# A two-layer encoder whose mixer order comes from a recorded plan: other prices for switches and narrow products, two other hand-over times

## The chip, the cores and the metric

The program runs on one core of one Trainium2 chip. The time is the device time of one execution in microseconds; the median of the runs is compared. The engines are TensorE (PE, with its weight loads as PEld), VectorE (DVE), ScalarE (ACT), GpSimd (POOL) and SyncE (SP, which issues most of the loads).

## The reference

The kernel computes two layers on a sequence of 512 positions and 1024 channels in float32, then a last RMS norm. `x` below is the residual stream.

```python
for layer in range(2):
    xn = rms_norm(x, mix_norm[layer])
    x = x + (fox_diff_mixer(xn) if layer == 0 else mlstm_mixer(xn))
    x = x + memory_cross_attention(rms_norm(x, ...), rms_norm(mem, ...), wq, wkv, wo)
    x = x + conv_ffn(rms_norm(x, ...), w_up, conv_w, conv_b, w_down)
return rms_norm(x, final_norm)
```

The first mixer has four heads of differential attention (two score maps each, one subtracted from the other) and eight heads of attention with a decay that is cumulated along the sequence; their outputs are joined and go through one output projection. The second mixer is an mLSTM of four heads. `mem` has 256 positions.

## The kernel before

Activations lie transposed: channels on the 128 partitions, the 512 positions along the free dimension, in eight tiles. Each float32 matrix product of a projection is made of three products of a faster kind (`float32r`): both operands are split into a rounded part and a rest (`wh` and `wl`, `xh` and `xl`), ACT casts the rounded part and DVE subtracts it (L655 is the line of the recording wrapper, so that nearly every instruction carries it, and tiles tell them apart). Loads of weights (`raw`) are issued by SP, three buffers deep.

Products of the other kind, plain float32, are few: transposes by the identity (`w<-ident,x`), probabilities times values (`w<-pt,v`) and some sums over columns. The text calls these narrow and the `float32r` products wide, as the planner does. The differential heads' `w<-pt,v` fill all 128 columns; those of the decaying heads come in pairs, two 64-column halves of the array, each with a `tile_position`.

A head of the first mixer runs like this. Two projections give queries and keys; DVE scales them (`tmp`), ACT and DVE write the parts `qa`, `ka`, `kb` in halves of 64 partitions. For each of four blocks of queries PE makes the scores (`s<-ka,qa`, `s<-kb,qa`) in one of two banks `s`; a DVE instruction (`x<-s,dmask` or `x<-s,tb`, named ISA in lists of the order and CUSTOM_DVE_ANT_0 in the trace) adds the mask or the decay and takes the row minimum, which frees the bank; ACT takes the exponential with its sum; DVE normalizes (`x<-x,sm`); PE transposes; DVE or ACT copies the result to `pt`; PE multiplies by the values. For the decaying heads POOL makes the mask (`tb<-fb`, an affine select) from the cumulated decays, which come from a chain of eight-row DVE instructions and a scan (`tmp<-ones,mem`) and go through memory (`decays`, `fb`). Meanwhile the memory input is prepared (`sq`, `sqt`, `mem`) for the cross-attention, and products of its key projection (`acc<-mem,wh`, `acc<-mem,wl`), which depend on nothing in the mixer, are put between the heads' work as fill. The heads' work ends at about 199 us on PE; the output projection (`acc<-mh,wh` and so on) follows.

The order of all this within a mixer is not written by hand. `Plan` first lays out the large steps by priorities (`PROJ`, `SOFT`). A `Recorder` notes every instruction that the steps issue, gives each a duration (`cost`), and hands the list to `Sched`, a list scheduler with one clock for each engine: `run` picks, engine by engine, the instruction that can start first or nearly so, by due times (`dues`). PE's tasks are due when the recorder's own clock reaches them, less an amount in `EARLIES` for each head. `again` first runs the schedule once and then makes PE's start times the due times of a second run. The instructions are then issued in the order found, and each engine carries its own out in that order. Times of the plan are used for nothing else: where the plan's clock is wrong, the chip waits.

For the prices, `cost` gives a wide product `MM * n / 512` with `MM = 0.216` us and a least value, and a narrow one four times that; a factor stands for products with a `tile_position`. In `Sched.run`, `self.kind` tells that the product before was narrow, `t.kinds` the kind of a task's first and last product, and `SWITCH = 0.083` us is what a change of kind adds. `DECAY_AT` is the time in the plan before which the decays' chain is not begun. Both mixers use these prices (the second has its own `EARLIES1` and no decays of this form).

Of the kernel before, what the change touches and what calls it, by code (L numbers as in the profile page):

```python
# [29 lines left out]
X_AT, X_STEP = 2.6, 0.6  # L30
WARM = 10
ROW_DMA, SPREAD_DMA, LATE = 2.7, 6.0, 12.0
DECAY_AT = 70
MEM_AT, MEM_STEP = (100, 20), (4.0, 4.0)
FILLS, FILL_AT, FILL_PRIO = 2, (130.0, 100.0), 99
FILL_DUE, FILL_LAST = ((215.0, None), (None, None)), (2, 0)
# [143 lines left out]
MM = 0.216  # L180
# [5 lines left out]
SWITCH = 0.083  # L186
# [14 lines left out]
PROJ = [10, 55, 30, 57, 64, 73, 73, 73]  # L201
SOFT = [-29, 17.5, 40.5, 23.0, 30.5, -4.5, 41.0, 156.5]
FV = [55]
EARLIES = [177.0, 102.0, 114.0, 56, 54.0, 114.0, 152, 57.0]
PROJ1, SOFT1, NORM1 = [1, -30, 20, 33], [3, 19.5, 30.5, 90], [0, 66.5, 79.5, 8.0]
GATE1, V1 = [33, 34, -24, 51], [-42, 20]
EARLIES1 = [30.0, 96.0, 105.0, 87.0, 60.0, 129.0, 90.0, 111.0]
# [9 lines left out]
class Sched:  # L217
# [66 lines left out]
    def run(self):  # L284
        if self.wait or self.exact:
            self.dues()
        order = sorted(self.tasks, key=lambda t: (t.prio, t.n))
        todo = {}
        want = {r: [] for r in self.slots}
        for t in order:  # L290
            todo.setdefault(t.eng, []).append(t)
        for t in self.tasks:
            for r, _ in t.take if not t.loose else ():
                want[r].append(t)
        now = {e: -self.ahead.get(e, 0.0) for e in todo}
        inf = float("inf")
        idle = 0.0
        while any(todo.values()):
            best = None
            for e, ts in todo.items():  # L300
                able = []
                for t in ts if e == "-" else ts[:300]:
                    at = max(t.after, -99.0 if e == "-" else now[e])
                    ok = True
                    for d in t.deps:
                        if d.end is None:
                            ok = False
                            break
                        at = max(at, d.end + (d.same if d.eng == e else d.lat))
                    if not ok:  # L310
                        continue
                    for j, (r, _) in enumerate(t.take):
                        if not t.loose and want[r][0] is not t:
                            ok = False
                            break
                        at = max(at, self.slots[r][self.slot(r, sum(a == r for a, _ in t.take[:j]))])
                    if not ok or at == inf:
                        continue
                    able.append((at, t))
                if able:  # L320
                    near = min(at for at, _ in able) + self.wait.get(e, 0.0) + 1e-6
                    soon, pick = next((at, t) for at, t in able if at <= near)
                    if best is None or soon < best[0]:
                        best = (soon, e, pick)
            assert best is not None, [(e, t.n, t.prio, [d.n for d in t.deps if d.end is None], t.take) for e, ts in todo.items() for t in ts[:3]]
            at, e, t = best
            todo[e].remove(t)
            if e == "PE":
                idle += at - now[e]
            if t.table and t.table != self.table:  # L330
                self.table, t.dur = t.table, t.dur + TABLE
            if t.kinds:
                if self.kind and t.kinds[0]:
                    t.dur += SWITCH
                self.kind = not t.kinds[1]
            t.start, t.end = at, at + t.dur
            now[e] = t.end
            for r, st in t.take:
                if not t.loose:
                    want[r].pop(0)  # L340
                s = self.slot(r)
                self.turn[r] += 1
                self.slots[r][s] = inf
                st["_" + r] = s
            for r, st in t.free:
                self.slots[r][st["_" + r]] = t.end + 0.1
            if t.fn:
                t.fn()
        self.now, self.idle = now, idle
# [108 lines left out]
class Recorder:  # L458
# [35 lines left out]
    def item(self, t, it):  # L494
        prio = it.prio
        self.last, self.it, it.tasks = None, it, []
        self.early = EARLIES[SOFT.index(prio)] if prio in SOFT and not self.layer else EARLIES1[(SOFT1 + NORM1).index(prio)] if self.layer and prio in SOFT1 + NORM1 else 0.0
        if self.direct and t >= self.at:
# [11 lines left out]
    def cost(self, eng, name, out, a, k):  # L510
        n = int(np.prod(out.shape[1:])) if not isinstance(out, View) or out.idx is not None else 0
        if name == "dma_start":
            return (0.0017 * n, 3.3) if eng == "sync" else (0.57 if eng == "gpsimd" else 0.36, 2.8 if n < 512 or out.shape[0] < P else 4.0)
        if eng == "tensor":
            if name == "transpose":
                return 0.109, 0.2
            rhs = k.get("rhs", a[2] if len(a) > 2 else None)
            n = int(np.prod(rhs.shape[1:]))
            wide = (rhs.ref.dtype if isinstance(rhs, View) else rhs.dtype) == F32R
            return (max(0.11, MM * n / 512) if wide else max(0.22, 4 * MM * n / 512)) * (0.7 if "tile_position" in k else 1.0), 0.2  # L520
        if eng == "vector":
            two = 0.065 + 1.06e-3 * n
            if name == "tensor_tensor_reduce":
                return two, 0.25
            if name == "scalar_tensor_tensor":
                return two + (0.06 if isinstance(k["scalar"], View) or not isinstance(k["scalar"], (int, float)) else 0.0), 0.25
            if name == "tensor_tensor":
                return two + (0.02 if n == 512 else 0.0), 0.25
            if name == "tensor_tensor_scan":
                return 1.13, 0.25  # L530
            if name in ("tensor_copy", "reciprocal"):
                return 0.07 + 1.03e-3 * n, 0.25
            if name == "tensor_scalar":
                return (0.07 if isinstance(k["scalar1"], float) else 0.135) + 0.53e-3 * n, 0.25
            if name == "tensor_reduce":
                return 0.2, 0.25
            return 0.1 + 0.85e-3 * n, 0.25
        if eng == "scalar":
            d = 0.1 + 0.83e-3 * n + (0.07 if name == "copy" and n == 512 else 0.0)
            if any(k.get(w) is not None and not isinstance(k[w], float) for w in ("scale", "bias")):  # L540
                d += 0.09
            if isinstance(out, View) and out.idx is not None and len(out.shape) == 3 and out.shape[2] == 4:
                d += 0.42
            return d + (0.1 if "accum_out" in k else 0.0), 0.25
        return {"affine_select": 0.14 + 0.85e-3 * n, "tensor_tensor": 1.3, "memset": 0.1}.get(name, 0.1), 0.25
# [143 lines left out]
class Builder:  # L689
# [630 lines left out]
    def mix0(self):  # L1320
        nc, t, tc = self.nc, self.t, self.tc
        with tc.tile_pool(name="mix0", bufs=1, reuse_waits="tile") as mp:
# [94 lines left out]
            g = self.p_gate(pl, lambda: gw, 40, gates, xk, [norm], 1)  # L1417
            g = pl.add(decays, 0, [g], 1, take=("ta", "ta"), free=("ta", "ta"), chain=(("A", 1.0), ("D", 0.6), ("A", 0.5), ("D", 3.4), ("-", ROW_DMA)), after=DECAY_AT)

# [1579 lines left out]
```

## Time and profile before

| | |
|---|---|
| median of 3 runs | 1389.02 us (1388.33 to 1389.69) |
| the profiled execution | 1388.45 us, span of its core 1386.7 us |
| PE busy | 1376.9 us (99%) |
| DVE, ACT, POOL busy | 1196.1, 883.6 and 153.3 us |
| granted TensorE clock | 1.00 throughout |

The page and the views give times in us from the start of the span. Matmuls overlap: a row's second number is how long a product took from its start to its modelled end, 0.38 us for 512 columns, while the next one starts 0.216 us later. Waits of PE therefore show as a distance between the starts of two rows that is longer than usual, and only for the longest as idle time in brackets.

### The profile page before, as it was taken

Reading aid. Unit: us, or ns where it says so; the run is one execution under the profiler, and the core shown is the slowest. Engines: PE = TensorE matmul, PEld = TensorE weight load, DVE = VectorE, ACT = ScalarE, POOL = GpSimd, SP = SyncE. Lnnn points to the kernel's source line nnn. Section 1 sums busy time; section 2 is a strip of 40 time slices with the busy share of each in tenths; the row PEclk is TensorE's granted clock in tenths of the full one; section 3 lists DMA queues with packets and bytes.
Section 4 is the critical chain, followed back from the end, with each engine's and each line's share of the span. In section 5 each row is a group of like instructions: output and inputs, shape, how many; then the busy total and the mean of one; then the engine's idle time right before and its main releaser. Section 6 shows DMA issues by size and latency. Waiting matters only on the chain.

```text
span 1386.7 us, 23590 instructions
## 1 busy us (share of the span) xinstructions
PE 1376.9 (99%) x8846; PEld 1263.1 (91%) x8846; DVE 1196.1 (86%) x2061; ACT 883.6 (64%) x1517; POOL 153.3 (11%) x213
## 2 busy tenths in 40 slices
PE   9999999999999999999999999999999999999998
PEld 8888888899899999999888889889989999999997
DVE  7887886887899999999768889678879999999984
ACT  7887764766667665666447675466656765665555
POOL 0012310010011111010001221001001111010000
PEclk9999999999999999999999999999999999999999
DMA  6243343865468777683353243477464887766622
GB/s 209 76 138 92 115 135 101 266 175 168 140 171 204 194 195 184 157 200 101 104 175 111 92 132 115 145 205 224 145 171 135 197 210 196 181 174 172 153 75 77
DMA packets 85410, 215.29 MB, mean 155 GB/s; under 512 B 11072, under 2 KB 11584, under 8 KB 85296
## 3 DMA queue, kind: packets, MB, share of 16 engines
q1 hardware_dynamic: 67104, 169.09, 37.0%
q0 software_dynamic: 15904, 43.44, 17.8%
q8 instruction: 69, 1.13, 0.3%
q10 hardware_dynamic: 2288, 1.26, 0.3%
q14 instruction: 45, 0.37, 0.1%
HBM read 205.30 MB, written 8.44 MB: 154 GB/s over the span
## 4 chain that ended last, share of the span: by engine, by line
PE 92%; DVE 6%; ACT 1%; issue 1%; POOLq 0%; ACTq 0%; DVEq 0%
PE acc L655 62%; PE w L655 17%; PE s L655 12%; DVE wl L655 1%; DVE x L655 1%; DVE sm L655 1%; DVE qc L655 1%; DVE f L655 1%; DVE va L655 1%; ACT ka L655 0%; ACT x L655 0%; DVE k L655 0%; DVE xe L655 0%; ACT qc L655 0%; DVE sa L655 0%
## 5 line engine op out<-in xcount | busy, mean ns | idle before, releaser
L655 ACT CAST wh<-raw 128x1024 fp32r<-128x1024 f32 (+2 forms) x218 | 222.2, 1022 | 154.2 <-PE acc L655 102.5
L655 DVE TENSOR_TENSOR wl<-raw,wh 128x1024 fp32r<-128x1024 f32 (+2 forms) x218 | 259.2, 1191 | 30.3 <-ACT wh L655 29.6
L655 PE MATMUL acc<-xh,wh 128*128 128x256 f32 (+1 forms) x704 | 228.8, 325 | 0.2 <-DVE x L655 0.2
L655 PE MATMUL acc<-xh,wl 128*128 128x256 f32 (+1 forms) x704 | 227.1, 323 | 0.0
L655 PE MATMUL acc<-xl,wh 128*128 128x256 f32 (+1 forms) x704 | 226.9, 322 | 0.0
L655 PEld LDWEIGHTS acc<-xh,wl 128*128 128x128 f32 x704 | 134.3, 191 | 8.5
L655 PEld LDWEIGHTS acc<-xh,wh 128*128 128x128 f32 x704 | 134.3, 191 | 8.3 <-DVE x L655 0.6
L655 PEld LDWEIGHTS acc<-xl,wh 128*128 128x128 f32 x704 | 134.4, 191 | 7.6
L655 DVE SCALAR_TENSOR_TENSOR qc<-va,vec,qc 128x512 f32<-128x512 f32 x176 | 131.8, 749 | 6.2 <-ACT qc L655 3.5
L655 PE MATMUL acc<-f,k 128*128 128x256 f32 x1008 | 126.1, 275 | 0.0
L655 PE MATMUL w<-q,wh 128*128 128x512 f32 x416 | 123.9, 380 | 0.3 <-ACT qc L655 0.3
L655 PEld LDWEIGHTS acc<-f,k 128*128 128x128 f32 x1008 | 121.5, 192 | 1.7
L655 PE MATMUL acc<-mem,wh 128*128 128x256 f32 (+1 forms) x472 | 103.2, 313 | 0.0
L655 ACT ACTIVATE qc<-va,vec 128x512 f32<-128x512 f32 x88 | 71.4, 814 | 32.1 <-DVE va L655 19.8
L655 ACT ACTIVATE u<-acc 128x256 f32<-128x256 f32 x96 | 36.6, 382 | 76.8 <-PE acc L655 70.7
L655 PEld LDWEIGHTS w<-q,wh 128*128 128x128 f32 x416 | 75.4, 190 | 9.5 <-ACT qc L655 0.7
L655 PEld LDWEIGHTS acc<-mem,wh 128*128 128x128 f32 x472 | 78.4, 191 | 4.7
L655 PE MATMUL w<-q,wl 128*128 128x512 f32 x208 | 78.9, 379 | 0.0
L655 PE MATMUL acc<-mem,wl 128*128 128x256 f32 (+1 forms) x236 | 73.8, 313 | 0.0
L655 DVE TENSOR_TENSOR x<-acc,x 128x512 f32<-128x512 f32 (+1 forms) x43 | 28.0, 654 | 47.5 <-PE acc L655 47.5
L655 PE MATMUL acc<-f,wh 128*128 128x256 f32 x384 | 66.8, 275 | 0.0
L655 PE MATMUL s<-f,wh 128*128 128x256 f32 x384 | 66.8, 275 | 0.0
(382 smaller groups left out, 3501.7 us busy)
## 6 DMA issues: line engine op xcount, KB each, us to landing
raw<-in_up_dram SPq DMA_DIRECT2D x46, 512.0 KB, 4.1
raw<-in_down_dram SPq DMA_DIRECT2D x32, 512.0 KB, 4.1
sa<-in_up_dram SPq DMA_DIRECT2D x28, 512.0 KB, 4.7
sa<-in_up_dram POOLq DMA_DIRECT2D x28, 512.0 KB, 6.3
vb<-in_up_dram SPq DMA_DIRECT2D x42, 256.0 KB, 3.9
xe<-in_up_dram POOLq DMA_DIRECT2D x42, 256.0 KB, 4.7
raw<-in_xk_dram SPq DMA_DIRECT2D x16, 512.0 KB, 3.9
raw<-in_wo_dram SPq DMA_DIRECT2D x16, 512.0 KB, 3.4
```

Source lines behind the costliest of these rows:

```text
L655: i = issue(*map(real, a), **{w: real(v) for w, v in k.items()})
```

## The change

Four things are edited. A switch of product kind costs the planner 0.083 us when PE goes from narrow to wide, as before, and now gives back 0.083 us when it goes from wide to narrow. The least duration of a wide product becomes 0.1115 us, and the factor for products with a `tile_position` 0.55 where it was 0.7. The decays may begin at 40 us in the plan where they could at 70. The third differential head's amount in `EARLIES` becomes 117 where it was 114.

```diff
-DECAY_AT = 70
+DECAY_AT = 40
...
-EARLIES = [177.0, 102.0, 114.0, 56, 54.0, 114.0, 152, 57.0]
+EARLIES = [177.0, 102.0, 117.0, 56, 54.0, 114.0, 152, 57.0]
...
             if t.kinds:
-                if self.kind and t.kinds[0]:
-                    t.dur += SWITCH
+                t.dur += SWITCH * ((self.kind and t.kinds[0]) - (not self.kind and not t.kinds[0]))
                 self.kind = not t.kinds[1]
...
-            return (max(0.11, MM * n / 512) if wide else max(0.22, 4 * MM * n / 512)) * (0.7 if "tile_position" in k else 1.0), 0.2
+            return (max(0.1115, MM * n / 512) if wide else max(0.22, 4 * MM * n / 512)) * (0.55 if "tile_position" in k else 1.0), 0.2
```

No instruction is added or removed on any engine; PE has 8756 products in both programs. PE's order is the same up to about 53 us of the trace and from about 199 us on; in the second mixer PE's order stays, and a handful of instructions on DVE, ACT, POOL and SP change places with a neighbour.

ACT, second differential head, at 56 to 62 us of the trace of before. The `ka` are its keys, `pt` the probabilities of the first head on their way to PE, `wh` a weight's rounded part, `sq`, `sqt` and `mem` the memory's preparation. First as it stood:

```order
L655 CAST wh_667<-raw_502 128x1024
L655 ACTIVATE sq_685<-raw_542 128x256
L655 ACTIVATE x_142<-x_142,sm_641 128x512
L655 CAST ka_126_692<-tmp_670 64x512
L655 CAST ka_127_700<-tmp_670 64x512
L655 CAST ka_126_692<-tmp_670 64x512
L655 CAST ka_127_700<-tmp_670 64x512
L655 ACTIVATE sqt_717<-raw_542 128x256
L655 ACTIVATE mem_722<-raw_542,vec 128x256
L655 COPY pt_633<-w_712 128x3x128
```

And as it stands after the change:

```order
L654 CAST ka_126_680<-tmp_674 64x512
L654 CAST ka_128_692<-tmp_674 64x512
L654 ACTIVATE x_142<-x_142,sm_648 128x512
L654 CAST ka_126_680<-tmp_674 64x512
L654 CAST ka_128_692<-tmp_674 64x512
L654 CAST wh_711<-raw_502 128x1024
L654 COPY pt_635<-w_716 128x3x128
L654 ACTIVATE x_136,sm_721<-x_136,sm_721 128x128
L654 ACTIVATE x_135,sm_731<-x_135,sm_731 128x128
L654 ACTIVATE sq_745<-raw_546 128x256
L654 ACTIVATE sqt_747<-raw_546 128x256
L654 ACTIVATE mem_751<-raw_546,vec 128x256
```

The three instructions of the memory's preparation went behind the copy to `pt`; the weight's cast stays ahead of it.

DVE, decaying heads, at 164 to 168 us. The ISA rows evict scores of the banks `s`, the row of `sm` behind each is its second half; `wl` is a weight's rest, `tmp<-acc` a scaled projection. As it stood:

```order
L655 ISA x_137,sm_1933<-s_1895,tb_1919 128x256
L655 ISA sm_1933 128x1
L655 RECIPROCAL sm_1880<-sm_1880 128x1
L655 COPY pt_1625<-w_1914 128x128
L655 TENSOR_SCALAR x_142<-x_142,sm_1880 128x512
L655 TENSOR_TENSOR wl_1952<-raw_1661,wh_1912 128x1024
L655 ISA x_139,sm_1965<-s_1949,tb_1937 128x384
L655 ISA sm_1965 128x1
L655 ISA x_140,sm_1969<-s_1954,tb_1944 128x512
```

After the change:

```order
L654 ISA x_139,sm_1937<-s_1893,tb_1930 128x256
L654 ISA sm_1937 128x1
L654 SCALAR_TENSOR_TENSOR tmp_1945<-acc_387_1817,rb_377 128x512
L654 COPY pt_1787<-w_1939 128x128
L654 ISA x_137,sm_1964<-s_1951,tb_1947 128x384
L654 ISA sm_1964 128x1
L654 ISA x_140,sm_1974<-s_1955,tb_1958 128x512
```

Between the eviction of 256 columns and that of 384 the weight's subtraction and a scaling of 512 columns are gone (they stand earlier now), and a scaled projection stands there.

PE, last decaying heads, at 185 to 188 us: scores among the fill. As it stood:

```order
L655 MATMUL acc_480_2245<-mem_807,wh_2109 128x256 x2
L655 MATMUL acc_480_2245<-mem_807,wl_2154 128x256
L655 MATMUL w_2270<-ident,x_141 128x128
L655 MATMUL acc_480_2245<-mem_820,wh_2109 128x256 x2
L655 MATMUL s_2266<-ka_455_2118,qa_435_2017 128x256
L655 MATMUL s_2266<-kb_112,qa_435_2017 128x256
```

After the change, from the last score ahead of such a place on:

```order
L654 MATMUL s_2232<-kb_114,qa_435_2024 128x256
L654 MATMUL acc_458_2128<-mem_837,wh_1915 128x256 x2
L654 MATMUL acc_458_2128<-mem_837,wl_2148 128x256
L654 MATMUL acc_458_2128<-mem_844,wh_1915 128x256 x2
L654 MATMUL acc_458_2128<-mem_844,wl_2148 128x256
L654 MATMUL acc_458_2128<-mem_889,wh_1915 128x256 x2
L654 MATMUL acc_458_2128<-mem_889,wl_2148 128x256
L654 MATMUL acc_458_2128<-mem_893,wh_1915 128x256 x2
L654 MATMUL acc_458_2128<-mem_893,wl_2148 128x256
L654 MATMUL w_2254<-ident,x_142 128x128 x2
```

More fill stands between a score and what follows it, and the transposes come in groups.

The scan of the decays, `tmp<-ones,mem` on DVE, moves from 71 us of the trace to a place that corresponds to 41 us, and POOL's `decays` and the first three `fb` with it.

## The prediction

> **What bounds the kernel now.** I read the page first: its busy times, its clock row and its chain.
>
> ```profile
> span 1386.7 us, 23590 instructions
> PE 1376.9 (99%) x8846; PEld 1263.1 (91%) x8846; DVE 1196.1 (86%) x2061; ACT 883.6 (64%) x1517; POOL 153.3 (11%) x213
> PEclk9999999999999999999999999999999999999999
> PE 92%; DVE 6%; ACT 1%; issue 1%; POOLq 0%; ACTq 0%; DVEq 0%
> ```
>
> PE is busy 99% of the span at the full clock, and the chain that ended last is PE for 92%. An order with the same products can therefore only gain what PE stands still for. Where that is, the table of windows tells, cut where the change has its stages:
>
> ```profile
> 16.00:100.00 84.00, 83.73 (x414) 70.94 (x413) 70.27 (x185) 68.28 (x140) 5.60 (x8) 1.00 0.35 110
> 100.00:160.00 60.00, 59.88 (x303) 52.21 (x304) 45.03 (x122) 43.73 (x92) 16.01 (x25) 1.00 0.30 90
> 160.00:214.00 54.00, 53.00 (x346) 42.73 (x346) 43.04 (x128) 33.26 (x77) 12.26 (x24) 1.00 0.43 134
> 667.00:884.00 217.00, 216.34 (x1094) 191.13 (x1093) 175.98 (x272) 126.58 (x195) 29.58 (x45) 1.00 0.40 129
> ```
>
> The first number is the window's length; behind it stand busy time and count of PE, PEld, DVE, ACT and POOL. PE's are 0.27, 0.12 and 1.00 us short of the length in the first mixer, 0.66 us in the second. This understates the waits, since a row's duration runs to its modelled end and the next product starts before it. I therefore went through the timeline of PE and compared each start with the usual distance to the next (0.216 us for 512 columns, 0.163 for 384, 0.11 for 256). Between 61.46 and 193.45 us of the first mixer 14 distances are at least 0.1 us too long, together 3.1 us; nine more are 0.05 to 0.09 us too long. All 23 make 3.7 us. That is the most that a better order of the first mixer's heads can give. These waits fall on 15 places (a product that waited makes the next one late by some 0.1 us as well, and I count the two together): 0.44 and 0.91 us at two of them, and 2.38 us at the other thirteen, 0.18 us on average.
>
> **The prices in the change.** First the switch of kind, from PE's timeline at 163 us, four transposes (narrow) and then wide products:
>
> ```profile
> 163.18 0.60 PE L655 MATMUL w<-ident,x 128*128 128x128 f32 x4
> 163.53 0.46 PE L655 MATMUL acc<-xh,wh 128*128 128x512 f32 x1
> 163.83 0.38 PE L655 MATMUL acc<-xl,wh 128*128 128x512 f32 x1
> ```
>
> The first wide product takes 0.30 us to the next start instead of 0.216: the 0.083 us of the plan. But the four transposes take 0.35 us, not four times 0.11: the last narrow one before a wide one is short by as much. A pair of switches is net nothing. So the changed rule says what the trace says, and the two switches that the order gains (87 from narrow to wide, 85 before) cost 0; if each were a loss of 0.083 us it would be 0.17 us, below what the rest can tell.
>
> Second, the products in two halves of 64 columns:
>
> ```profile
> 171.31 0.33 PE L655 MATMUL s<-kb,qa 128*128 128x384 f32 x1
> 171.57 2.38 PE L655 MATMUL w<-pt,v 128*64 128x512 f32 x16
> 173.87 0.43 PE L655 MATMUL s<-ka,qa 128*128 128x384 f32 x1
> ```
>
> Sixteen of them take 2.30 us to the next start. At `MM` for four-pass products they would be 4.33 us undiscounted (0.864, 0.648, 0.432 and 0.22, in two halves), so the old factor 0.7 says 3.03 and the new one 2.38: this price was 0.65 us too long at each of four groups, 2.6 us, and the old switch charge added 0.083 us for each of the mixer's 56 switches into narrow work or out of it that it over-counted, 4.6 us. The old plan's clock thus ran some 7 us behind the chip's toward the end of the heads, just where the waits lie. These are prices: they change nothing on the chip by themselves. The 384-column score at 171.31 also keeps PE for 0.26 us instead of 0.163 before the half-array products start, at all four groups; the groups stay four, so this 0.1 us each stays.
>
> On a rule against this change: the Trainium skill, "TensorEngine Tiling (Array Packing)", section Key Properties, says that a change of tiling mode makes the array drain. The trace agrees for the half-array products (the 0.26 us above). Applied to every change of product kind as well it would make the two new switches cost 0.17 us; the rows at 163 us show no net loss there.
>
> **The change part by part.** *Scan, `decays` and `fb`, 71 to 41 us.* The scan takes 1.20 us of DVE at 70.97. It goes into DVE's idle time at 41 us; POOL's row stands first:
>
> ```profile
> L655 POOL DMA_DIRECT2D decays<-tmp x1 | 0.7, 719 | 52.6 <-DVE tmp L655 52.6
> 39.83 1.40 DVE L655 TENSOR_TENSOR qa<-tmp,qa 64x512 fp32r<-64x512 f32 x2
> 42.28 0.69 DVE L655 TENSOR_TENSOR tmp<-acc,rb 128x512 f32<-128x512 f32 x1 [1.04 <-PE acc L655]
> ```
>
> DVE waits 1.04 us there for PE, so the cost is 0, at most the 0.2 us by which it is longer. POOL was idle for 52.6 us before its `decays`, so this transfer and the three `fb` loads pass no one's work. At the old place it lay here:
>
> ```profile
> 70.97 1.20 DVE L655 TENSOR_TENSOR_SCAN tmp<-ones,mem 8x512 f32<-8x512 f32 x1
> 74.66 0.38 PE L655 MATMUL acc<-xh,wl 128*128 128x512 f32 x1
> 74.92 0.38 PE L655 MATMUL s<-ka,qa 128*128 128x256 f32 x1
> ```
>
> From 74 to 80 us PE's scores start behind DVE's evictions in six distances that are 0.55 us too long in all (the first here 0.26 instead of 0.216). DVE has 1.2 us less to do ahead of them; I take 0.3 us gained, between 0 and 0.55, since the evictions among themselves stay as close. SP's loads change by one place for one load of the memory and four for one load of `wo`: neither is waited for at these places.
>
> *Copy to `pt` at 62 us.* PE, then ACT:
>
> ```profile
> 61.46 0.28 PE L655 MATMUL s<-kb,qa 128*128 128x256 f32 x1
> 62.00 2.42 PE L655 MATMUL w<-pt,v 128*128 128x512 f32 x8 [0.27 <-ACT pt L655]
> 57.09 0.41 ACT L655 ACTIVATE sq<-raw 128x256 f32<-128x256 f32 x1
> 60.75 0.42 ACT L655 ACTIVATE sqt<-raw 128x256 f32<-128x256 f32 x1
> 61.07 0.49 ACT L655 ACTIVATE mem<-raw,vec 128x256 fp32r<-128x256 f32 x1
> 61.47 0.48 ACT L655 COPY pt<-w 128x384 f32<-128x384 f32 x1
> ```
>
> PE waits 0.54 - 0.11 = 0.44 us for the copy. Three instructions that go behind it take 0.41 + 0.42 + 0.49 us, 1.1 to 1.2 us with their overlap. The copy is over that much earlier if its own bank is ready; 0.44 us goes.
>
> *Second copy, 132 us.*
>
> ```profile
> 132.03 0.28 PE L655 MATMUL s<-kb,qa 128*128 128x256 f32 x1
> 132.43 0.38 PE L655 MATMUL s<-ka,qa 128*128 128x256 f32 x1
> 126.16 0.60 ACT L655 CAST mh<-ta 128x512 fp32r<-128x512 f32 x1
> 126.67 1.22 ACT L655 ACTIVATE x<-x,sm 128x384 f32<-128x384 f32 x2
> ```
>
> The score at 132.43 starts 0.40 us after the one ahead, 0.28 too late, and the next 0.1. The cast of `mh`, 0.51 us to the next start, goes behind the casts of the keys that these scores wait for; `mh` is not read before the output projection. 0.39 us goes.
>
> *Longest wait, 167 us.*
>
> ```profile
> 166.75 0.38 PE L655 MATMUL acc<-xh,wl 128*128 128x512 f32 x1
> 167.80 0.35 PE L655 MATMUL s<-ka,qa 128*128 128x256 f32 x1 [0.68 <-DVE sm L655]
> 165.15 0.90 DVE L655 TENSOR_SCALAR x<-x,sm 128x512 f32<-128x512 f32 x1
> 165.97 1.21 DVE L655 TENSOR_TENSOR wl<-raw,wh 128x1024 fp32r<-128x1024 f32 x1
> 167.10 0.54 DVE L655 CUSTOM_DVE_ANT_0 x<-s,tb 128x384 f32<-128x384 f32 x1
> ```
>
> The score stands for 0.84 us more than its 0.216, and 0.07 follow: 0.91 us. It needs a bank that the eviction at 167.10 frees. Ahead of that eviction stand the scaling of 512 columns (0.82 us to the next start) and the weight's subtraction (1.13 us), 1.95 us. In the new order a scaled projection of 512 columns stands there, 0.69 us by the row at 42.28 above (it has one operand more, so this is an estimate); the small copy is there in both. The eviction comes some 1.26 us earlier, more than the wait: 0.91 us goes.
>
> *176 to 199 us.* Scores and transposes among the fill; the last of the distances:
>
> ```profile
> 193.10 0.27 PE L655 MATMUL acc<-mem,wh 128*128 128x256 f32 x1
> 193.45 0.48 PE L655 MATMUL s<-ka,qa 128*128 128x512 f32 x1
> ```
>
> (0.35 instead of 0.11.) From 176.64 on eleven distances make 1.45 us. With more fill between a score and what needs it I take half, 0.7 us, between 0 and 1.45.
>
> *New waits.* A different order also puts products close behind what makes their operands. I find five such places in the order, at what were 54, 60, 91, 128 and 172 us, and price each as the thirteen lesser waits of before: 5 x 0.18 = 0.9 us. The bounds are 0 and 2.0 us (eleven of them).
>
> The second mixer keeps PE's order; neighbours that change places on the other engines have 0.66 us of idle PE to move: 0, within 0.2. Waits outside the heads stay.
>
> **Sum.** 0.3 + 0.44 + 0.39 + 0.91 + 0.7 = 2.74 us gone, 0.9 us new: 1.8 us less. The profiled execution has 1388.45 us (span 1386.7 and 1.75 around it) and would have 1386.6; the median of the runs lies 0.57 us above it, so 1389.02 - 1.8 = 1387.2 us.
>
> **The rivals.** *All waits of the heads go and none comes:* 3.7 us less, 1385.3 us. For it: every price now is as measured, so the plan sees each wait. Against: the plan knows no wait between engines to the tenth of a microsecond, and 43.04 us of DVE in the last 54 leave it nearly as full as before. Chance 0.14.
>
> *The waits move and don't shrink:* 1389.0 us. For it: in every stage DVE and ACT have the same work, and five new close places are seen already. Against: the three longest waits have each a cause that the new order removes. Chance 0.16.
>
> *Slower, by DVE and POOL meeting.* The scaling at 165.15 took 0.90 us beside POOL's making of a mask; the same scaling alone, at 162.50, took 0.49:
>
> ```profile
> 164.69 1.07 POOL L655 TENSOR_SCALAR_AFFINE_SELECT tb<-fb 128x384 f32<-128x384 f32 x2 [2.77 <-DVE sm L655]
> 162.50 0.49 DVE L655 TENSOR_SCALAR x<-x,sm 128x512 f32<-128x512 f32 x1
> L655 DVE TENSOR_SCALAR x<-x,sm 128x512 f32<-128x512 f32 x8 | 4.3, 534 | 0.1
> ```
>
> If the new order puts scalings beside masks, ahead of evictions that scores wait for, each costs 0.41 us. From five on (2.05 us) it eats the gain; at twelve (4.9 us) the time is 1389.0 - 1.8 + 4.9 = 1392.1 us. Against: the eight scalings of 512 columns took 534 ns on average, 44 above the one alone, 0.35 us together, one such meeting in eight; twelve in the mixer's 32 is far from that. Chance 0.04. The Trainium skill, "SBUF — State Buffer", section Who interferes with whom, states that a DVE instruction of this kind in its two-port mode and one of GpSimd shut each other out for a whole instruction; the 0.90 beside 0.49 us agrees.
>
> **How the numbers follow.** The forecast keeps 0.66. Its own range is 2.7 to 0.7 us of gain, 1386.3 to 1388.3 us, with half a microsecond for a median of three runs that lie 1.4 us apart. To hold eight in ten I reach toward both neighbours: 1385.5 to 1388.8 us. About 0.2% (2.8 us) is what a measurement of this kernel can tell from no change. Faster by more than that needs 1386.2 or less: the first rival and the edge of the forecast, 0.18. Slower by more: the last rival, 0.03 of it. The rest is 0.79.
>
> **What would show it.** In the profile after: the window from 160 to 214 us with under 0.6 us of idle PE; no wait over 0.2 us ahead of the first `w<-pt,v` of 512 columns in the differential heads, and none over 0.3 us ahead of a score behind two evictions on DVE; the scan at about 41 us without a wait of PE behind it; the first layer's output projection starting 1.8 us earlier and the distance from there to the end unchanged. I am wrong if the output projection starts when it did (the second rival), if scalings of 0.8 us and more stand in rows ahead of waiting scores (the third), or if the time moves behind 245 us.

## The result, and the profile after

The changed kernel takes 1386.39 us (median of 18 runs, 1386.06 to 1387.13) against 1388.67 us before (18 runs): 2.3 us less, ratio 0.9984 with a 95% interval of 0.9976 to 0.9991. The forecast was 1.8 us less. The page of its profiled execution, which answers to the one of before:

```profile
span 1384.5 us, 23592 instructions
PE 1376.1 (99%) x8846; PEld 1262.5 (91%) x8846; DVE 1196.0 (86%) x2061; ACT 883.5 (64%) x1517; POOL 152.9 (11%) x213
PEclk9999999999999999999999999999999999999999
PE 94%; DVE 4%; issue 0%; ACT 0%; POOLq 0%; ACTq 0%; DVEq 0%
```

The busy times are the same; the span is 2.2 us shorter and the chain has two points less of DVE. The windows (length, then busy time and count of PE, PEld, DVE, ACT, POOL) show where:

```profile
16.00:100.00 84.00, 84.00 (x416) 71.95 (x415) 70.88 (x185) 69.07 (x140) 5.61 (x8) 1.00 0.36 117
100.00:160.00 60.00, 59.98 (x305) 52.00 (x304) 45.85 (x123) 44.17 (x92) 15.08 (x24) 1.00 0.27 80
160.00:214.00 54.00, 53.84 (x352) 43.71 (x351) 44.29 (x131) 34.66 (x80) 13.05 (x25) 1.00 0.41 136
```

PE was 0.27, 0.12 and 1.00 us short of these three lengths; now it is 0.00, 0.02 and 0.16. The output projection's first product on PE, in the trace of before and then in that of after:

```profile
198.76 0.38 PE L655 MATMUL acc<-mh,wh 128*128 128x512 f32 x1
```

```profile
196.73 0.38 PE L654 MATMUL acc<-mh,wh 128*128 128x512 f32 x1
```

It starts 2.03 us earlier. From a product of the output projection at 214.21 us (212.19 after) to PE's last product it takes 1166.34 us before and 1166.38 after: the whole gain lies in the first mixer's heads.

By the same reading as in the prediction, the distances on PE that are 0.05 us or more too long between 53 and 203 us sum to 1.49 us; they were 3.73. The largest that are left, first at 164 us (PE, DVE, POOL):

```profile
164.21 0.60 PE L654 MATMUL w<-ident,x 128*128 128x128 f32 x4
164.79 0.43 PE L654 MATMUL s<-ka,qa 128*128 128x384 f32 x1
...
163.65 0.76 DVE L654 TENSOR_TENSOR kb<-tmp,ka 64x512 fp32r<-64x512 f32 x1
164.44 0.29 DVE L654 CUSTOM_DVE_ANT_0 x<-s,tb 128x128 f32<-128x128 f32 x1
...
163.57 2.30 POOL L654 TENSOR_SCALAR_AFFINE_SELECT tb<-fb 128x128 f32<-128x128 f32 x4 [2.28 <-DMA fb<-decays]
```

Four transposes took 0.35 us elsewhere and the score comes 0.58 us behind their start. It waits for the bank that the eviction at 164.44 frees. That one needs the first of POOL's four masks and starts right behind DVE's subtraction `kb`, which ends at 164.41. POOL had stood 2.28 us for its load `fb` (issued from 159.09 us on), but its first mask took 0.29 us from 163.57 and was ready at 163.86: in this execution DVE's own work came last, and not the load. Then at 172 and 181 us:

```profile
172.43 0.33 PE L654 MATMUL s<-kb,qa 128*128 128x384 f32 x1
172.77 0.44 PE L654 MATMUL w<-ident,x 128*128 128x128 f32 x2
...
181.32 0.28 PE L654 MATMUL s<-kb,qa 128*128 128x256 f32 x1
181.61 0.38 PE L654 MATMUL s<-ka,qa 128*128 128x256 f32 x1
```

0.34 instead of 0.163 and 0.29 instead of 0.11. At 62 us no wait is left: the products with `pt` follow the score by 0.11 us.

```profile
61.38 0.28 PE L654 MATMUL s<-kb,qa 128*128 128x256 f32 x1
61.49 1.73 PE L654 MATMUL w<-pt,v 128*128 128x512 f32 x4
```

And the scan on DVE stands where it was expected, and no wait of PE follows it up to 54 us:

```profile
41.40 1.21 DVE L654 TENSOR_TENSOR_SCAN tmp<-ones,mem 8x512 f32<-8x512 f32 x1
42.54 0.65 DVE L654 TENSOR_TENSOR tmp<-acc,rb 128x512 f32<-128x512 f32 x1
```

### The profile page after: what moved, and what is told of

Its sections match the earlier page's. It is cut to its first block, busy times and chain, and to the rows that moved or that the text cites. A ratio compares the mean times of both kernels' runs of the same rounds, so it can differ in the third digit from the quotient of the medians.

```text
span 1384.5 us, 23592 instructions
## 1 busy us (share of the span) xinstructions
PE 1376.1 (99%) x8846; PEld 1262.5 (91%) x8846; DVE 1196.0 (86%) x2061; ACT 883.5 (64%) x1517; POOL 152.9 (11%) x213
## 4 chain that ended last, share of the span: by engine, by line
PE 94%; DVE 4%; issue 0%; ACT 0%; POOLq 0%; ACTq 0%; DVEq 0%
PE acc L654 64%; PE w L654 18%; PE s L654 13%; DVE qc L654 1%; DVE sm L654 1%; DVE wl L654 1%; DVE f L654 1%; DVE va L654 1%; DVE k L654 0%; DVE xe L654 0%; DVE x L654 0%; ACT qc L654 0%; DVE sa L654 0%; DVE q L654 0%; DVE u L654 0%
```

## The experiments

All but e8, which has its own section, in one table. *Waits* are sums of PE's distances that are 0.05 us or more too long, by place of the trace; *heads* is the time between two products that stand in the same place of all these programs (14.29 and 214.21 us in the trace of before), against before's 199.92; these are from one profile each. *Median* is against the kernel before on the same chip, with the ratio's interval. The heads are read to hundredths, but of one execution each: they and the medians differ by up to 1.1 us (e2's profiled execution was its fastest, 1.28 us below its median). The experiments' medians have intervals of 1.2 us on either side.

| kernel | 53-82 | 82-164 | 164-176 | 176-203 | all | heads | median | ratio |
|---|---|---|---|---|---|---|---|---|
| before | 0.98 | 0.39 | 0.91 | 1.44 | 3.73 | 0 | 0 | |
| the change | 0.28 | 0.24 | 0.63 | 0.33 | 1.49 | -2.15 | -2.28 | 0.9976 to 0.9991 |
| e1 lengths only | 0.94 | 0.40 | 1.17 | 0.27 | 2.77 | -1.07 | -0.53 | 0.9986 to 1.0004 |
| e2 switch only | 0.37 | 0.65 | 1.09 | 1.95 | 4.07 | +0.56 | +1.68 | 1.0004 to 1.0022 |
| e3 decays only | 0.74 | 0.44 | 0.95 | 1.44 | 3.57 | -0.21 | +0.11 | 0.9991 to 1.0009 |
| e4 without lengths | 0.28 | 0.24 | 1.04 | 1.95 | 3.52 | 0.00 | -0.13 | 0.9991 to 1.0008 |
| e5 without switch | 0.74 | 0.44 | 1.22 | 0.26 | 2.65 | -1.27 | -1.79 | 0.9977 to 0.9996 |
| e6 without decays | 0.38 | 0.67 | 0.80 | 0.34 | 2.19 | -1.44 | -0.54 | 0.9988 to 1.0005 |
| e7 moved by hand | 2.19 | 0.10 | 0.64 | 1.43 | 4.37 | +0.68 | +1.04 | 0.9995 to 1.0013 |
| e9 factor 0.53 | 0.28 | 0.24 | 0.91 | 0.12 | 1.56 | -2.14 | -2.81 | 0.9973 to 0.9991 |
| e10 factor 0.62 | 0.28 | 0.25 | 1.37 | 0.76 | 2.65 | -0.85 | -1.23 | 0.9983 to 1.0001 |
| e11 0.53, transpose 0.112 | 0.89 | 0.33 | 1.21 | 0.63 | 3.04 | -0.43 | -1.00 | 0.9985 to 1.0003 |
| e12 0.53, slower DVE | 0.68 | 0.28 | 0.07 | 0.06 | 1.09 | -2.65 | -2.40 | 0.9976 to 0.9994 |

The third head's amount in `EARLIES` needs no run: with 117 in the kernel before, and with 114 in the changed one, the program that comes out is the same to the last instruction. It does nothing.

### One part alone (e1 to e3), and two parts without the third (e4 to e6)

The theory on trial is the prediction's: the plan's clock is too slow by the sum of its wrong prices, and each price that is mended takes its share.

e1, from before:

```diff
-max(0.11, MM * n / 512) ... (0.7 if "tile_position" in k else 1.0)
+max(0.1115, MM * n / 512) ... (0.55 if "tile_position" in k else 1.0)
```

> Only the lengths of narrow products are changed (0.55 and 0.1115). Theory of the prediction, shares: the waits come from a plan whose clock is too slow by 7 us, of which this price is 2.6 us; it takes its share of the waits behind 100 us, some 0.6 us less than before, and the scan at 71 us keeps the 0.55 us at 74 to 80 us. Rival, place: the waits that the change removes lie where the half-array products are (160 to 200 us), so this price does nearly all of it: 1.1 us less or more, all behind 160 us. Rival, scan: the early scan does it, and this kernel stays within 0.2 us of before.

e2, from before:

```diff
-                if self.kind and t.kinds[0]:
-                    t.dur += SWITCH
+                t.dur += SWITCH * ((self.kind and t.kinds[0]) - (not self.kind and not t.kinds[0]))
```

> Only the switch's charge is made net nothing. Theory of the prediction, shares: this price is 4.6 of the 7 us by which the plan's clock is wrong, so it takes most of the waits behind 100 us: some 1.0 us less than before. Rival, place: the clock's error as such does not matter, the order of neighbours does; a corrected switch beside narrow products that are still too long gives another order with as many waits, between no change and 0.8 us slower. Rival, scan: within 0.2 us of before.

e3, from before:

```diff
-DECAY_AT = 70
+DECAY_AT = 40
```

> Only the decays' chain may begin at 40 us. Theory of the prediction: 0.3 us less, all of it at 74 to 80 us, and the waits at 62, 132, 167 and 176 to 199 us stay as they were, since nothing of them hangs on the scan. Rival, scan: the scan's 1.2 us of DVE set off everything behind it, and this kernel has the whole gain, 2 us or more. Rival, chaos: moving one instruction gives another order behind 80 us as well, and the waits there come out elsewhere, anything from 0.7 us less to 0.7 us more than before.

e4, from the changed kernel:

```diff
-max(0.1115, MM * n / 512) ... (0.55 if "tile_position" in k else 1.0)
+max(0.11, MM * n / 512) ... (0.7 if "tile_position" in k else 1.0)
```

> The change without the lengths of narrow products (switch, decays and the third head's amount stay). Theory of the prediction, shares: 4.6 of 7 us of the clock are mended and the scan is early: 1.3 to 1.6 us less than before. Rival, place: without the half-array price nothing is gained behind 160 us, and what the early scan gives is lost again to the other order: within 0.3 us of before.

The shares fell with e2 and e4. (e1 and e3 do not decide by their totals: e1's median is at the 0.6 us of the shares and its heads at the 1.1 us of the rival; e3's heads give 0.21 us for 0.3, but the wait at 62 us, which was to stay, is gone, and at 73 to 77 us there is as much as before, 0.63 us.) The switch's rule, to which I had given 4.6 of 7 us, makes the kernel slower when it comes alone. The two largest waits of its heads, on PE:

```profile
172.20 0.38 PE L654 MATMUL acc<-xl,wh 128*128 128x512 f32 x1
173.12 0.43 PE L654 MATMUL s<-ka,qa 128*128 128x384 f32 x1 [0.54 <-DVE sm L654]
...
198.23 0.44 PE L654 MATMUL w<-ident,x 128*128 128x128 f32 x2
199.27 0.48 PE L654 MATMUL acc<-mh,wh 128*128 128x512 f32 x1 [0.60 <-ACT wh L654]
```

The first score stands 0.70 us too long, the output projection's first product 0.85 us (its weight is not cast yet). e4, with the early scan as well, has the same two waits to 0.01 us, and the change does not have them. The three parts do not add up: -1.07, +0.56 and -0.21 us of heads make -0.72, and together they give -2.15.

e5 and e6, from the changed kernel, fill the scheme of all combinations (each with the lines of e2 or e3 turned back):

```diff
-                t.dur += SWITCH * ((self.kind and t.kinds[0]) - (not self.kind and not t.kinds[0]))
+                if self.kind and t.kinds[0]:
+                    t.dur += SWITCH
```

> The change without the switch's rule (lengths of narrow products and the decays' time stay). Theory of the prediction, shares of the clock's error: 4.6 of the 7 us stay, so 0.7 to 0.9 us less than before. Rival after the first four runs, lengths: waits stand behind the half-array groups because the plan reckons these too long, and with the lengths right the switch's rule is worth nothing: 1.7 to 2.2 us less than before, the place at 172 us, 191 and 198 us without the waits of 0.70, 0.44 and 0.85 us that the switch alone shows.

```diff
-DECAY_AT = 40
+DECAY_AT = 70
```

> The change without the decays' time (both prices stay, the scan stays at 71 us). Theory of the prediction: 0.3 us of the gain are gone, 1.7 to 2.0 us less than before. Rival, lengths: the scan's place costs 0.5 us in every pair of kernels that differ in it alone, so 1.3 to 1.7 us less than before. Rival, scan as a condition: without it the places at 54 to 80 us are as in before, and no more than 1.0 us is gained.

The columns of the table tell what each part does, better than the totals. The lengths act behind 176 us: 0.26 to 0.34 us of waits with them, 1.44 or 1.95 without, whatever the rest. The pairs that differ in the decays alone (before and e3, e1 and e5, e2 and e4, the change and e6) have one order of PE there, and their waits agree to 0.01 us: there the waits belong to the order and not to the execution. (The lengths are two edits, the factor and the least duration of a wide product, and no run has one without the other; the fill behind 176 us is made of products that the second one touches.) From 53 to 82 us the switch's rule and the early scan act, and only both give 0.28 (0.37 and 0.74 alone, 0.98 with neither). From 164 to 176 us no single part helps. With the lengths right, the switch's rule is worth 0.88 us of heads beside the early scan and 0.37 without; with wrong lengths it costs 0.56 alone and 0.21 beside the early scan. The early scan, for which the sum had 0.3 us, is worth 0.71 us of heads beside both prices, 0.56 beside the switch and 0.2 alone or beside the lengths. My second guess, that the switch is worth nothing beside right lengths, is half borne out: e5 lost the waits at 191 and 198 us as it said, but has 0.42 us at 170 to 171 us, and its heads gained 1.27 us, not 1.7 or more. Its median gained 1.79 us, which is within the guess. e6's heads (-1.44 us) lie where the lengths' rival put them, its median (-0.54) where the scan's did; both miss the 1.7 to 2.0 us of the prediction. The medians of e5 and e6 do not separate the theories: their intervals overlap.

### Three pieces moved by hand (e7)

The prediction priced three waits by what stands ahead of the instruction that PE waits for. e7 leaves the plan of before as it is and moves only those pieces, in the list that the plan has made (numbers are tasks):

```diff
+MOVES = [([314, 317, 318, 315, 316, 319, 320, 323, 324], 165), ([477], 585), ([476], 491), ([696, 706], 734)]
...
+        for moved, behind in self.moves if seq else ():
+            at = [i for i, t in enumerate(seq) if t.n in moved]
+            to = next(i for i, t in enumerate(seq) if t.n == behind)
+            block, between = [seq[i] for i in at], [t for t in seq[at[0]:to + 1] if t.n not in moved]
...
+            seq[at[0]:to + 1] = between + block
```

> The kernel before, with three pieces moved after the plan is made and nothing else: at 62 us the memory's preparation (sq, sqt, mem on ACT with their four DVE instructions) goes behind the copy to pt, at 132 us the cast and the subtraction of mh go behind the casts of the keys, at 167 us the scaling and the weight's subtraction on DVE go behind the two evictions. Theory of the prediction, each wait by what stands ahead of it on its engine: 0.44, 0.39 and 0.91 us gone, 1.7 us less than before. Rival at 62 us: ACT's copy waits for DVE's copy into the same tile, which ends at 61.44 us, so the 0.44 us stays, and the preparation on DVE then costs at 74 us what it does not cost at 62. Rival for all, conservation: DVE has the same work before the next place, so what a piece gives is taken back at the next wait (74 us, 171 to 176 us), and the kernel is within 0.5 us of before.

At 62 us the wait stayed: 0.44 us, as before. ACT's row and DVE's say why:

```profile
62.00 0.48 ACT L667 COPY pt<-w 128x384 f32<-128x384 f32 x1 [0.75 <-DVE pt L667]
...
61.67 0.29 DVE L667 COPY pt<-w 128x128 f32<-128x128 f32 x1
```

ACT now stands idle for 0.75 us: its copy waits for DVE's copy into another part of the same tile, behind two subtractions of `kb`. In the trace of before ACT was busy up to the copy, and so the work ahead of it looked like the cause. The other traces agree: where the second subtraction of `kb` starts after 60.4 us (before, e1, e7, e11) the wait is 0.39 to 0.44 us, and where it starts by 59.7 us (the change, e2 to e6, e9, e10) there is none. What went wrong behind it, at 74 us:

```profile
74.09 0.38 PE L667 MATMUL acc<-xh,wl 128*128 128x512 f32 x1
75.08 0.38 PE L667 MATMUL s<-ka,qa 128*128 128x256 f32 x1 [0.61 <-ACT ka L667]
```

The score comes 0.78 us late. It waits for keys that ACT casts from a scaling on DVE (72.41 us), and the memory's preparation, which cost nothing at 62 us, now stands further up on DVE, ahead of two evictions:

```profile
66.36 0.42 DVE L667 TENSOR_TENSOR sq<-sq,sqt 128x256 f32<-128x256 f32 x1 [1.03 <-ACT sqt L667]
66.76 1.28 DVE L667 SCALAR_TENSOR_TENSOR mem<-raw,vec,mem 128x256 fp32r<-128x256 f32 x3
```

DVE stands 1.03 us for ACT's part of it and then works 1.6 us on its own. From the eviction behind it (67.96 us, 65.90 in the trace of before) to the scaling (72.41 and 70.36) everything is 2.05 us later than before, while PE is only 0.53 us later.

At 132 us the cast of `mh` was the cause: 0.39 us before, 0.15 now (the table counts 0.10 of it, the rest is under its 0.05). At 167 us the wait is gone altogether (0.91 before, none now), and then this (PE, DVE, POOL):

```profile
170.05 0.28 PE L667 MATMUL s<-kb,qa 128*128 128x256 f32 x1
170.64 0.35 PE L667 MATMUL s<-ka,qa 128*128 128x256 f32 x1 [0.31 <-DVE sm L667]
...
168.50 1.66 DVE L667 TENSOR_TENSOR wl<-raw,wh 128x1024 fp32r<-128x1024 f32 x1
...
168.15 0.93 POOL L667 TENSOR_SCALAR_AFFINE_SELECT tb<-fb 128x128 f32<-128x128 f32 x2
```

The subtraction that was moved behind the evictions now stands ahead of the next ones, and beside POOL's masks it takes 1.66 us: 0.54 us of wait with the product behind it. In the trace of before the group of these subtractions has this row (busy time, mean ns, idle time ahead):

```profile
L655 DVE TENSOR_TENSOR wl<-raw,wh 128x1024 fp32r<-128x1024 f32 x30 | 36.6, 1221 | 11.3 <-ACT wh L655 11.3
```

Not every meeting costs as much: in the first mixer of before four of these subtractions overlap a mask and take 1.22 to 1.31 us. Two of them had begun first, and there the mask was the one that took long (1.33 us for 256 columns at 137.50 us, 0.39 for the one at 168.69 us here).

Of the 0.91 us, 0.64 is back by 176 us, and from there on the waits sum to 1.43 us for 1.44 before, at partly other places. The Trainium skill, "SBUF — State Buffer", Who interferes with whom, has a DVE instruction with two inputs in SBUF contend with GpSimd's reads; the 1.66 us agrees.

### The prices themselves (e8)

Products that nothing reads are put before the first weights; only the lengths of their blocks are read.

```diff
...
+        for few, many in ((turn, 2), (half, 4)):
+            n = 64 // many
+            for apart in (False, True):
+                for _ in range(n if apart else 1):
+                    for _ in range(1 if apart else n):
+                        few()
+                    for _ in range(many if apart else 64):
+                        wide()
```

> The kernel before with products that nothing reads, before the first weights: 32 transposes and then 64 wide products of 512 columns, the same again with two wide products behind each transpose, then 16 pairs of plain float32 half-array products of 256 columns and 64 wide ones, the same again with four wide ones behind each pair. Only the lengths of the four blocks are read. Theory (a switch pair is net nothing): the second block is as long as the first within 0.3 us. Rival (each switch drains): 31 more pairs at 0.083 us make it 2.6 us longer. For the half-array pairs, theory from the row at 171.31 us: 15 more entries at 0.09 us, 1.4 us longer; rival (nothing to pay): 0; rival (in and out): 2.8 us.

The blocks on PE, with the alternating ones cut to their first and last rows (32 and 16 repeats; the trace has two records for each half-array product):

```profile
10.94 3.66 PE L655 MATMUL acc<-ident 128*128 128x128 f32 x32
14.35 14.80 PE L655 MATMUL acc<-wh 128*128 128x512 f32 x64
29.00 0.27 PE L655 MATMUL acc<-ident 128*128 128x128 f32 x1
29.02 0.71 PE L655 MATMUL acc<-wh 128*128 128x512 f32 x2
...
46.70 0.27 PE L655 MATMUL acc<-ident 128*128 128x128 f32 x1
...
47.37 7.13 PE L655 MATMUL acc<-wh,ones 128*64 128x256 f32 x64
54.43 14.84 PE L655 MATMUL acc<-wh 128*128 128x512 f32 x64
69.20 0.65 PE L655 MATMUL acc<-wh,ones 128*64 128x256 f32 x4
...
94.82 0.65 PE L655 MATMUL acc<-wh,ones 128*64 128x256 f32 x4
```

Grouped, 32 transposes and 64 wide products take 29.00 - 10.94 = 18.06 us. Alternating, 31 periods take 46.70 - 29.00 = 17.70 us, 32 of them 18.27: 0.2 us more for 31 more pairs of switches, 0.007 us a pair where a drain on each would give 0.083. A lone transpose takes 0.02 us to the next start and the wide product behind it is late by the rest. For the half-array pairs theory and both rivals fell: grouped 69.20 - 47.37 = 21.83 us, alternating (94.82 - 69.20) / 15 x 16 = 27.33 us, 5.5 us more for 15 visits. Each visit to the half array and back costs 0.37 us, not 0.09: about 0.10 us on the wide product ahead, 0.05 between the first two pairs of records, 0.10 on the last pair and 0.11 on the wide product behind. The group at 171.57 us of before has the same four (0.09, 0.05, 0.10 and 0.10 us; the score at 173.87 us keeps PE for 0.27 instead of 0.163). The prediction had read only the first.

### How much hangs on exact prices (e9 to e12)

After e1 to e7 the rival was scatter: each set of prices draws another order, and its waits fall anywhere. Four small edits of the changed kernel:

e9:

```diff
-... (0.55 if "tile_position" in k else 1.0)
+... (0.53 if "tile_position" in k else 1.0)
```

> The changed kernel with the factor of half-array products at 0.53, which is what the rows give (2.30 of 4.33 us). Theory, true lengths: the plan gets nearer to the chip by 0.09 us at each of four groups, 0 to 0.4 us less than the changed kernel, so 2.2 to 2.7 us less than before. Rival, scatter: each set of prices draws another order, and this one lands anywhere between 1.0 and 2.7 us less than before.

e10:

```diff
-... (0.55 if "tile_position" in k else 1.0)
+... (0.62 if "tile_position" in k else 1.0)
```

> The changed kernel with the factor at 0.62: the plan reckons a group 0.39 us too long, where 0.70 reckons 0.73 too long and 0.55 reckons 0.08. Theory, true lengths in proportion: about half of what the wrong length costs is back, the waits from 189 to 203 us are some 0.8 us (1.75 with 0.70, none with 0.55), 1.0 to 1.3 us less than before. Rival, threshold: the order behind the groups flips at one price between 0.62 and 0.70, so nothing waits there and 1.7 to 2.2 us are gained. Rival, scatter: the waits come elsewhere, 1.0 to 2.7 us less than before.

e11, with e9's line:

```diff
-                return 0.109, 0.2
+                return 0.112, 0.2
```

> The kernel with factor 0.53, and a transpose reckoned at 0.112 us instead of 0.109; the chip's own are between 0.109 and 0.112. Theory, true lengths: 3 ns on some hundred transposes are 0.3 us over the whole mixer, so the same time as with 0.109 within 0.2 us. Rival, scatter: the order is drawn anew, and as much as 1.2 us of the gain may go, 1.0 to 2.5 us less than before.

e12, with e9's line:

```diff
-            two = 0.065 + 1.06e-3 * n
+            two = 0.1 + 1.06e-3 * n
```

> The kernel with factor 0.53, and each two-operand DVE instruction reckoned 0.035 us longer than it is. Theory, true lengths: a price that was right is made wrong by 4 to 6% on DVE's longest work, so the waits grow, 0.5 us or more slower than with the right price. Rival, margin: a plan that thinks DVE slower puts PE's products further behind their evictions, the waits shrink below 1.2 us in all, 2.3 to 2.9 us less than before. Rival, scatter: 1.0 to 2.7 us less.

e11 decides against true lengths: 3 ns on a transpose take 1.7 us of e9's 2.14 back in the heads, and the medians of these two are 1.81 us apart. e10 has no wait behind 189 us, so the proportion that I expected there is refuted, but 1.2 us more than the change between 164 and 203 (some 0.6 of it is the late load told below). And e12, with a price that is wrong by its own measure, has the fewest waits of all (1.09 us) and the shortest heads. That is what its rival *margin* foretold; one order is too few to tell it from scatter. Its median does not show it in full. In its profiled execution a late load of a weight cost PE 0.37 and 1.04 us at 931 us, in a part that the change does not reach, so one profile is not enough to say whether that is its order's doing. The best median is e9's, 1386.31 us, 2.81 us below its own runs of before where the change is 2.28 below; that is no difference that these intervals can tell.

One place also moves by itself. e10 and e9 have the change's order on all engines up to 168 us, and the score that follows the four transposes there was 0.23 us late in the change, 0.53 in e9 and 0.80 in e10. POOL and PE of e10:

```profile
164.69 1.79 POOL L654 TENSOR_SCALAR_AFFINE_SELECT tb<-fb 128x128 f32<-128x128 f32 x4 [3.38 <-DMA fb<-decays]
...
165.37 0.43 PE L654 MATMUL s<-ka,qa 128*128 128x384 f32 x1 [0.55 <-DVE sm L654]
```

POOL's load landed 1.1 us later than in the profile of the change, though it was issued at the same time (159.10 us). Half of that is hidden behind DVE's `kb`, as the rows of the change showed. So 0.6 us of any column from 164 to 176, and of any total, may be the load's chance and not the order's.

## Why the prediction was right, and where not

**The size and the sign** held: 2.28 us less, 1.8 forecast, and in the heads alone. The sum by terms, from the trace: gone are 0.44 at 62 us (0.44 predicted), 0.45 at 74 to 80 (0.3), 0.39 at 132 (0.39), 0.91 at 167 (0.91) and 1.11 from 176 on (0.7), 3.30 us for 2.74; new are 0.06 at 54, 0.12 at 60, 0.19 at 128, 0.06 at 162, 0.30 at 164 and 0.34 at 172 us, 1.07 us for 0.9. Four of the five places named for new waits have one, the one at 91 us does not, and those at 162 and 164 us were not named. The 0.7 us from 176 on was half of what stood there, taken without a reason from the rows, and 0.3 us was too little for the scan. That the rest came out so near is in part luck: the heads gained between 0.43 and 2.65 us with the neighbouring prices of e9 to e12.

**At 62 us the step was wrong and its number right.** "The copy is over that much earlier if its own bank is ready" failed on another condition, the other engine's copy into the same tile. The wait went because DVE's two subtractions of `kb`, at 59.72 us before, stand 2.1 us earlier after the change. e7 shows the cause; that the earlier `kb` is what removed the wait is read from the traces alone, since no run moves only that.

**At 132 us** step and size held; e7 shows the cast to be 0.24 us of the 0.39. **At 167 us** cause and size held, shown by e7, but the step named no next wait: in the change 0.30 us stand at the two scores of 164.79 and 165.22 us, behind other work of DVE's (`kb`), and in e9 and e10 behind POOL's load of `fb`.

**The clock of the plan** was the step that failed as a reason. The 7 us is itself too much: PE's timeline of before goes from narrow to wide 36 times ahead of the output projection, and the old rule charged only these: 3.0 us, not 4.6 for 56 switches. And that the clock was slow "just where the waits lie" does not say what a mended price gives: the switch, the larger share, gave a loss alone (e2), and e11 shows that 3 ns can draw an order with 1.5 us more waits (e9 beside e11; 0.3 of it may be the load's chance). What holds is narrower: with half-array products reckoned 0.73 us too long a group, every order has 1.4 us or more of waits behind 176 us (before, e2, e3, e4, e7), and with lengths within 0.4 us none of the eight kernels has more than 0.8. Apart from e7's moves by hand these are only two different orders of PE on the one side and six on the other, so it is likely, and not shown, that the lengths do it.

**The switch of kind** as a price is shown: net nothing (e8). The rule of the Trainium skill, "TensorEngine Tiling (Array Packing)", Key Properties, on mode switches, weighed in the prediction, holds for half-array products, by more than I read from one row. The kernel has four groups of them before and after, so the sum did not notice.

**The rivals.** All waits gone: 1.49 us are left. Waits that only move: this is what e3 and e4 are, a change of order with 3.6 and 3.5 us of waits, and e7 in part; its chance of 0.16 was fair only for all parts together. DVE meeting POOL: the eight scalings of 512 columns went from 534 to 485 ns on average, so the mechanism worked for the change by a little (the one of 0.90 us is gone); that it also hits the longer subtractions (e7) I had not reckoned with.

## What to carry to other kernels

When a recorded order is drawn again from other prices, forecast the waits that can go and expect new ones for a part of them (here 2.24 of 3.73 us stayed gone, and in the other orders that the plan drew between -0.34 and 2.64); a gain of this size belongs to the one order that was drawn, and the neighbouring price may not have it. What stands ahead of a late instruction on its own engine is its cause only if nothing on another engine ends at the same time: look there before pricing the move, above all where two engines write parts of one tile. The same holds the other way: an engine that stood long for a load need not be the last to be ready. And a piece of work that is moved out of the way of one wait should be followed to the next wait on the same engine, which is where it comes due.

## What the runs showed of the hardware

A change between plain float32 transposes and `float32r` products costs next to nothing net (0.007 us a pair, 31 pairs): the 0.083 us late start behind the wide product is time that the narrow one did not take. A visit of two half-array products among full ones costs 0.37 us (15 visits, 5.5 us), four times what the one row ahead of a group showed. DVE's subtraction of 1024 columns took 1.66 us beside two masks of POOL, the first of which had begun before it, where its mean was 1.22; begun before the mask it kept 1.22 us and the mask took 1.33. Two engines that copy into different parts of one tile went one after the other (ACT idle for 0.75 us), by the order that the program keeps between them. The landing of one load moved a score by 0.6 us between three programs of the same order up to that place.
